# Feed-forward stage of a two-layer encoder: earlier weight requests, a later transpose, and two orders kept

## The chip, the core and the metric

The kernel runs on one core of a Trainium2 chip. The metric is the device time of one execution in microseconds (us). A core has a matrix engine (TensorE, PE in the profile), a vector engine (VectorE, DVE), a scalar engine (ScalarE, ACT), GpSimd (POOL) and SyncE (SP), which issues most DMA transfers, one after the other. Each engine works through its own list of instructions in order; semaphores hold an instruction until what it needs is done.

## The reference, cut to what matters

```
for i in range(2):
    mix = mla_mixer(h) if i == 0 else diff_mixer(h)
    h = layernorm(ALPHA * h + mix)
    h = layernorm(ALPHA * h + (silu(gate) * up) @ w_down)    # gate, up = split(h @ w_gu, 2)
```

Sequence 1024, model width 1024, feed-forward width 2816, all float32. The change lies in the feed-forward part, `silu(gate) * up` and the product with `w_down`, of both layers.

## The kernel before, in words

**The planner.** The kernel is written in a framework that orders the instructions itself: a planner simulates the engines and takes, for each engine, the instruction of the highest priority that is ready by its own clock. Priority is the order in the source, raised by `tc.high_priority`. `behind(i, j)` adds an edge without a semaphore: `i` comes after `j` in the order of the engine that both are on. Buffers come from pools with a number of slots for each tag; a load waits for a slot. The large tiles (tag `big`) have 6 slots, shared by raw gate weights (`gr`), results of the first gate products (`pg`), `hp` and `sh`, which hold finished units on their way to DRAM.

**Precision.** TensorE multiplies in a rounded form. Each operand is split in a high part (a cast on ScalarE) and a low part (a subtraction on VectorE or GpSimd), and a product is three matmuls: high by high, low by high and high by low. `op_unit` (L508 to L516) makes such a pair for a weight; the pairs of the gate stage rotate through tags `wh` and `wl`, 3 slots each. A product of 128 x 512 by 512 inner elements is 4 x 3 = 12 matmuls (`product`, L547 to L557).

**The gate stage** (`ffn` from L521). There are 22 units n, in `order`, each a 128-column block of gate or up weights and its products. The 2 x 2 block product is done in seven products instead of eight, by sums and differences of blocks. Products "1" and "2" go to accumulator `ga`, "6", "7" and "4" to `gb`, "5" and "3" to `gc`. Their inputs are xo, t1, t2, t3, t4 and b22, made of the transposed activations. For units 0 to 5 products "1" and "2" come first, from weights loaded separately (`load_pre`, `gates`), and their results `pg` of units 2 to 5 go to DRAM and come back into `tmp` (L655). The others follow in `stream`: for units 0 and 1 products 5, 3 and then 6, 7, 4; for units 2 to 5 the products 6, 7, 5, 4, 3; from unit 6 on 1, 6, 2, 7, 5, 4, 3. `prepare(n, pr)` forms a weight (sums and differences on VectorE, L585 to L593) and splits it; `consume(n, pr)` does the product, and then VectorE adds the accumulator to the unit's partial sums (L633 to L645), which frees the accumulator for the next product. `prepare` runs 4 positions of the stream ahead of `consume` in the source; the planner may run it further ahead. `load(n)` (L559 to L563) fetches a unit's raw weights, 1024 KB.

**Before the gate stage.** The last row block of the attention output is normalised, transposed on TensorE and put into the block sums by `raw_x` (L463 to L486). That is left over as `pending`, and called inside `ffn` at high priority (L690), after the first `gates(0)`.

**The down stage** (from L737 on) multiplies the finished units with `w_down` in seven blocks, each of 132 matmuls (`whole`, L843), their operands coming from `from_h` and from `b11`, `t1`, `t2` and others. `t2` forms two differences on VectorE for each of 11 steps (L805).

Until the change, only the last unit's products (n = 21) are kept in source order on TensorE (L555).

Of the kernel before, what the change touches and what calls it, by code (L numbers as in the profile page):

```python
# [12 lines left out]
ALU = mybir.AluOpType  # L13
# [3 lines left out]
P = 128  # L17
# [25 lines left out]
def trunk(  # L43
# [103 lines left out]
    def tr(ps_out, in_):  # L147
        T.transpose(ps_out, in_, ident)

# [135 lines left out]
    def out_proj(side, w_o, o_dram, x_src, x_dst, lng, lnb, xo):  # L285


        with tc.tile_pool(name="op0", bufs=2, side=side, reuse_waits="tile") as pool:
# [21 lines left out]
            for tb in LAST_ORDER:  # L310
# [34 lines left out]
                prev = (tb, y)  # L345
        return lambda: raw_x(prev[1], xo, prev[0], f"a0_{prev[0]}")

    class OutProj:
# [95 lines left out]
        def rest(self, lng, lnb, xo):  # L444
# [15 lines left out]
            self.st.close()  # L460
            return lambda: raw_x(self.z[prev], xo, prev, f"a1_{prev}")

    def raw_x(y, xo, tb, name):  # L463

# [56 lines left out]
    def ffn(side, xo, xst, pending, layer, x_src, x_dst, lng, lnb, next_x, spare=()):  # L521
# [25 lines left out]
        def product(n, o, w, x, first):  # L547
            for k in range(4):
                kc = slice(k * P, (k + 1) * P)
                for a, b in ((0, 0), (0, 1), (1, 0)):  # L550
# [14 lines left out]
        def load_pre(n, eng):  # L565
# [4 lines left out]
            for i, pr in enumerate("12"):  # L570
                ops[n, pr] = op_unit(t[:, i], eng, f"gp{layer}_{n}_{pr}")

        begun = set()

        def prepare(n, pr):


            if n not in begun:
                begun.add(n)
                load(n + 1)  # L580
                if n < npre - 1:
                    load(n + 2)
            a11, a12, a21, a22 = (r[n][:, i] for i in range(4))
            if pr == ("5" if n < 2 else "6"):
                V.tensor_tensor(a21, a21, a22, ALU.add)  # L585
            if pr == ("3" if n < 2 else "6"):
                V.tensor_tensor(a11, a21, a11, ALU.subtract)
            if pr == "3":
                V.tensor_tensor(a12, a12, a11, ALU.subtract)
            s3 = None  # L590
            if pr == "7":
                s3 = wp.tile([P, 2, 512], F32, tag="wr", name=f"s3_{layer}_{n}", bufs=2)[:, 0]
                V.tensor_tensor(s3, a22, a11, ALU.subtract)  # L593
            src, eng = {
# [3 lines left out]
            eng = V if n < 2 else eng  # L598
            ops[n, pr] = op_unit(src, eng, f"g{layer}_{n}_{pr}")

        def consume(n, pr):
# [3 lines left out]
            if pr in "12":  # L605
# [26 lines left out]
            if pr == "6":  # L632
                V.tensor_tensor(u2, p1, acc[n, "b"], ALU.add)  # L633
                for c in acc[n, "cs"] if n < 2 else ():
                    V.tensor_tensor(u2, u2, c, ALU.add)
            elif pr == "7":
                V.tensor_tensor(u3, p1, acc[n, "b"], ALU.add)  # L637
                if n < 2:
                    V.tensor_tensor(u3, u3, acc[n, "cs"][0], ALU.add)
            elif pr == "5":  # L640
                V.tensor_tensor(u3, u3, acc[n, "c"], ALU.add)  # L641
            elif pr == "4":
                V.tensor_tensor(p1, p1, acc[n, "b"], ALU.add)
            else:
                V.tensor_tensor(u2, u2, acc[n, "c"], ALU.add)  # L645
            if pr == ("4" if n < 2 else "3"):
# [69 lines left out]
        gates(4)  # L716
        load(2)
        for u in stream[:2]:
            prepare(*u)
# [44 lines left out]
        def from_h(s, name, tags=tags, late=False):  # L764

            for gi, (j0, j1) in enumerate(thirds):
# [803 lines left out]
```

## Time and profile before

| what | value |
|---|---|
| median of 3 runs | 2277.39 us (2275.31 to 2277.57) |
| profiled execution, its time | 2276.84 us |
| its span, first to last instruction | 2275.1 us |
| mean granted TensorE clock | 0.996 |
| PE busy | 98% of the span |
| DVE, ACT, POOL busy | 69%, 45%, 38% |

Busy is the time in which an engine runs an instruction. In a timeline row the first number is the start in us from the span's start, the second the duration; what stands in brackets at the end is the idle time of that engine ahead of the instruction, and what ended it. `op_g`, `op_gp`, `op_h` and `op_w` are weight or activation pairs; `gr` are raw gate weights. L551 is the matmul of the gate stage, L843 that of the down stage. A row of the stretches view gives the stretch, its length, then for each engine busy time and count of instructions, then the granted clock, the DMA engines' share and GB/s. The gate stage runs from about 443 to 872 us in layer 0, and from about 1624 to 2055 us in layer 1.

### The profile page before, as it was taken

Reading aid. Unit: us, or ns where it says so; the run is one execution under the profiler, and the core shown is the slowest. Engines: PE = TensorE matmul, PEld = TensorE weight load, DVE = VectorE, ACT = ScalarE, POOL = GpSimd, SP = SyncE. Lnnn points to the kernel's source line nnn. Section 1 sums busy time; section 2 is a strip of 40 time slices with the busy share of each in tenths; the row PEclk is TensorE's granted clock in tenths of the full one; section 3 lists DMA queues with packets and bytes.
Section 4 is the critical chain, followed back from the end, with each engine's and each line's share of the span. In section 5 each row is a group of like instructions: output and inputs, shape, how many; then the busy total and the mean of one; then the engine's idle time right before and its main releaser. Section 6 shows DMA issues by size and latency. Waiting matters only on the chain.

```text
span 2275.1 us, 31209 instructions
## 1 busy us (share of the span) xinstructions
PE 2238.8 (98%) x11410; PEld 1915.3 (84%) x11410; DVE 1569.9 (69%) x2848; ACT 1022.1 (45%) x2115; POOL 869.2 (38%) x693
## 2 busy tenths in 40 slices
PE   8999999999999999999999999999999999999998
PEld 8899998887888888888889898987778888888886
DVE  5676665696666667878576667677786656658878
ACT  4455664342333333445465656555432333334444
POOL 2232341113444444656333534322014444445551
PEclk9999999999999999999999999999999999999999
DMA  5010115443535338454311212054343223238453
GB/s 203 14 35 31 51 61 188 145 156 103 183 128 195 125 130 324 176 199 148 103 44 32 70 33 67 20 202 167 111 171 117 92 102 107 100 124 311 164 180 149
DMA packets 110443, 287.77 MB, mean 126 GB/s; under 512 B 8513, under 2 KB 30657, under 8 KB 99793
## 3 DMA queue, kind: packets, MB, share of 16 engines
q1 hardware_dynamic: 105872, 275.35, 34.2%
q0 software_dynamic: 4416, 10.42, 1.7%
q8 instruction: 90, 1.47, 0.3%
q14 instruction: 65, 0.52, 0.1%
HBM read 204.47 MB, written 77.07 MB: 124 GB/s over the span
## 4 chain that ended last, share of the span: by engine, by line
PE 87%; DVE 6%; DMA 3%; issue 2%; ACT 1%; POOL 1%; SPq 0%; DVEq 0%; POOLq 0%; ACTq 0%
PE gb L551 14%; PE gc L551 10%; PE ga L551 8%; PE dw L843 6%; PE zp_a L417 4%; PE s_a L219 4%; PE s_b L219 3%; PE dv L843 3%; PE bp L143 3%; PE bp L145 3%; PE dx L843 3%; PE bp L144 3%; PE dy L843 2%; PE o_a L262 2%; PE o_b L262 2%
## 5 line engine op out<-in xcount | busy, mean ns | idle before, releaser
L514 ACT CAST op_g<-gr 128x512 fp32r<-128x512 f32 x240 | 146.8, 621 | 378.6 <-PE gb L551 185.3
L515 POOL TENSOR_TENSOR op_g<-gr,op_g 128x512 fp32r<-128x512 f32 x104 | 145.7, 1406 | 248.7 <-ACT op_g L514 144.5
L515 DVE TENSOR_TENSOR op_h<-rh,op_h 128x512 fp32r<-128x512 f32 x152 | 169.5, 1144 | 48.3 <-ACT op_h L514 48.3
L551 PE MATMUL ga<-xh_m,op_g 128*128 128x512 f32 x512 | 168.3, 389 | 0.0
L514 ACT CAST op_h<-rh 128x512 fp32r<-128x512 f32 x152 | 92.6, 620 | 152.0 <-PE dx L843 50.4
L843 PE MATMUL dw<-op_w_t,op_h 128*128 128x512 f32 x660 | 151.6, 390 | 0.6 <-DVE op_h L515 0.6
L843 PEld LDWEIGHTS dw<-op_w_t,op_h 128*128 128x128 f32 x660 | 123.6, 188 | 26.8 <-DVE op_h L515 1.4
L515 POOL TENSOR_TENSOR op_w_t<-tt,op_w_t 128x512 fp32r<-128x512 f32 x66 | 101.8, 1551 | 84.5 <-ACT op_w_t L514 83.0
L227 ACT ACTIVATE l_b<-l_b,mx_b 128x256 f32<-128x256 f32 (+7 forms) x128 | 99.4, 777 | 66.8 <-DVE mx_b L222 65.3
L515 DVE TENSOR_TENSOR op_g<-gr,op_g 128x512 fp32r<-128x512 f32 x136 | 112.6, 832 | 16.9 <-ACT op_g L514 16.6
L515 POOL TENSOR_TENSOR op_g<-s,op_g 128x512 fp32r<-128x512 f32 x40 | 55.1, 1376 | 179.5 <-ACT op_g L514 171.4
L551 PE MATMUL gb<-t3h_f,op_g 128*128 128x512 f32 x352 | 117.9, 397 | 5.5 <-DVE tmp L633 5.5
L843 PE MATMUL dx<-op_w_b,op_h 128*128 128x512 f32 x528 | 121.1, 390 | 0.8 <-DVE op_w_b L515 0.8
L1367 POOL TENSOR_SCALAR l_b<-l_b,rb,cst 128x128 f32<-128x128 f32 (+3 forms) x64 | 52.6, 821 | 179.2 <-DVE rb L1366 171.8
L843 PEld LDWEIGHTS dx<-op_w_b,op_h 128*128 128x128 f32 x528 | 98.9, 188 | 22.4 <-DVE op_w_b L515 1.7
L551 PE MATMUL gb<-t4h_f,op_g 128*128 128x512 f32 x352 | 115.7, 390 | 1.3 <-DVE tmp L637 1.3
L551 PE MATMUL gc<-b22h_f,op_g 128*128 128x512 f32 x352 | 115.8, 390 | 0.8 <-DVE tmp L641 0.6
L551 PE MATMUL gb<-t2h_f,op_g 128*128 128x512 f32 x352 | 115.7, 390 | 0.4 <-DVE op_g L515 0.4
L551 PE MATMUL gc<-t1h_f,op_g 128*128 128x512 f32 x352 | 115.9, 390 | 0.0
L551 PEld LDWEIGHTS ga<-xh_m,op_g 128*128 128x128 f32 x512 | 96.2, 188 | 19.9
L143 PE MATMUL bp<-xT_f,h_wb 128*128 128x512 f32 x256 | 100.8, 394 | 0.1
L145 PE MATMUL bp<-xT_f,l_wb 128*128 128x512 f32 x256 | 100.7, 393 | 0.0
(391 smaller groups left out, 6753.5 us busy)
## 6 DMA issues: line engine op xcount, KB each, us to landing
gr<-in_w_gu SPq DMA_DIRECT2D x44, 1024.0 KB, 6.8
rh<-h_dr SPq DMA_DIRECT2D x28, 1024.0 KB, 4.9
h_dr<-sh SPq DMA_DIRECT2D x22, 1024.0 KB, 4.9
h_dr<-hp SPq DMA_DIRECT2D x22, 768.0 KB, 4.1
tt<-in_w_dn SPq DMA_DIRECT2D x44, 256.0 KB, 6.3
wo_dr<-op_pwo SPq DMA_DIRECT2D x16, 512.0 KB, 3.4
z<-xs_dr SPq DMA_DIRECT2D x16, 512.0 KB, 8.2
rw_b<-in_w_dn SPq DMA_DIRECT2D x8, 1024.0 KB, 7.7
```

The source lines that it names most:

```text
L143: T.matmul(ps_out, lh, rh, start=(i == 0), stop=False)
L144: T.matmul(ps_out, lh, rl, start=False, stop=False)
L145: T.matmul(ps_out, ll, rh, start=False, stop=(i == n - 1))
L219: T.matmul(s[:, :w], lh, rh[:, ks], start=(j == 0), stop=(j == len(q_pass) - 1))
L227: ends["exp"] = A.activation(l[:, :n], l[:, :n], AF.Exp, bias=mx, scale=-1.0, accum_out=sm).ins
L262: T.matmul(po[:, c], a, b[:, j % 2, c], start=st, stop=sp_, skip_group_check=True)
L417: T.matmul(m, a[:, h, :], self.wo[h][w][:, c], start=(start and h == heads[0] and a is oh and w == 0), stop=(stop and h == heads[-1] and a ...
L514: turns["hi"] = A.copy(t[:, 0], src).ins
L515: turns["last"] = eng.tensor_tensor(t[:, 1], src, f32(t[:, 0]), ALU.subtract).ins
L551: i = T.matmul(o, w[:, a, kc], x[b][:, k, :], start=(first and k == 0 and (a, b) == (0, 0)), stop=(k == 3 and a == 1), skip_group_check=Tr ...
L843: T.matmul(o, h[:, a, c], w[:, b_], start=(first and (a, b_) == (0, 0)), stop=(last and a == 1), skip_group_check=True,).ins for a, b_ in ...
L1367: G.tensor_scalar(l1[:, :n], l1[:, :n], r[:, 1:2], nlam, ALU.mult, ALU.mult)
```

## The change

It has five parts, all in the feed-forward part or in what it calls.

- **Loads.** `prepare(n)` asks for units n+1 and n+2, and up to unit 3 also for n+3. Before, it asked for n+1, and up to unit 4 also for n+2.
- **Last row block, layer 1.** In layer 1 only the weights of units 0 and 1 are loaded ahead of `gates(0)`, and those of 2 and 3 behind it in the source. The first transpose of each half of the last row block is put behind the last product of `gates(0)`. Unit 3's weight casts on ScalarE come behind the copy of the last "1" product.
- **VectorE's lead.** The operations that form weights go through `formed`, the sums through `added_up`. The first forming operations stand behind the last operation of `raw_x`; from step 10 of the stream on, those of position i+4 stand behind the sum of position i-6.
- **Last units.** The products of units 20 and 21 keep the source's order on TensorE, not only those of 21.
- **Down stage.** `t2`'s differences stand behind the split of the same step's `h`.

```diff
     def tr(ps_out, in_):
-        T.transpose(ps_out, in_, ident)
+        return T.transpose(ps_out, in_, ident).ins
...
-            return lambda: raw_x(self.z[prev], xo, prev, f"a1_{prev}")
+            return lambda after: raw_x(self.z[prev], xo, prev, f"a1_{prev}", after)
...
-                tr(pt[:, k * P:(k + 1) * P], y[:, (4 * kh + k) * P:(4 * kh + k + 1) * P])
+                i = tr(pt[:, k * P:(k + 1) * P], y[:, (4 * kh + k) * P:(4 * kh + k + 1) * P])
+                if k == 0 and after is not None:
+                    behind(i, after)
...
-            V.tensor_tensor(b21, b21, b12, ALU.add)
+            return V.tensor_tensor(b21, b21, b12, ALU.add).ins
...
-                    if n == NFF - 1 and k == 0 and (a, b) == (0, 0) and "product" in ends:
+                    if n >= 20 and k == 0 and (a, b) == (0, 0) and "product" in ends:
                         behind(i, ends["product"])
...
                 ops[n, pr] = op_unit(t[:, i], eng, f"gp{layer}_{n}_{pr}")
+                if layer and n == 3:
+                    behind(turns["hi"], ends["p1"])
 
-        begun = set()
+        begun, summed, allowed = set(), [], []
+
+        def formed(*args):
+            i = V.tensor_tensor(*args).ins
+            if allowed:
+                behind(i, allowed[-1])
...
                 load(n + 1)
-                if n < npre - 1:
-                    load(n + 2)
+                load(n + 2)
+                if n < npre - 2:
+                    load(n + 3)
...
+        def added_up(*args):
+            summed.append(V.tensor_tensor(*args).ins)
...
                 if pr == "1":
-                    A.copy(p1, acc[n, "a"])
+                    ends["p1"] = A.copy(p1, acc[n, "a"]).ins
...
-        for n in range(4):
+        for n in range(4 - 2 * layer):
             load_pre(n, G if n < 2 else V)
         gates(0)
+        for n in range(4 - 2 * layer, 4):
+            load_pre(n, V)
         load(0)
         load(1)
         with tc.high_priority(40):
-            pending()
+            turned = pending(ends["product"])
...
+        allowed.append(turned)
...
+        marks = []
         for i, u in enumerate(stream):
+            if i >= 6 and marks[i - 6]:
+                allowed.append(marks[i - 6])
             if i + ahead < len(stream):
                 prepare(*stream[i + ahead])
             consume(*u)
+            marks.append(summed[-1] if summed else None)
...
                 t = op_unit(src, V, f"h{layer}_{name}_{j}", tags, pool)
+                turns["h"] = turns["last"]
...
                 for i in range(2):
-                    V.tensor_tensor(tt[j][:, i], r, tt[j][:, i], ALU.subtract)
+                    behind(V.tensor_tensor(tt[j][:, i], r, tt[j][:, i], ALU.subtract).ins, turns["h"])
```

In `prepare` and `consume`, `V.tensor_tensor` becomes `formed` in the forming operations and `added_up` in the sums. In layer 0 `raw_x` is called without `after`.

More of the change, by code (lines that the diff above doesn't have):

```diff
@@ L345, in out_proj @@
                 prev = (tb, y)
-        return lambda: raw_x(prev[1], xo, prev[0], f"a0_{prev[0]}")
+        return lambda after: raw_x(prev[1], xo, prev[0], f"a0_{prev[0]}")
     class OutProj:
@@ L460, in rest, with raw_x @@
             self.st.close()
-            return lambda: raw_x(self.z[prev], xo, prev, f"a1_{prev}")
-    def raw_x(y, xo, tb, name):
+            return lambda after: raw_x(self.z[prev], xo, prev, f"a1_{prev}", after)
+    def raw_x(y, xo, tb, name, after=None):
         c = slice((tb % 4) * P, (tb % 4) * P + P)
@@ L580, in prepare @@
                 load(n + 1)
-                if n < npre - 1:
-                    load(n + 2)
+                load(n + 2)
+                if n < npre - 2:
+                    load(n + 3)
             a11, a12, a21, a22 = (r[n][:, i] for i in range(4))
             if pr == ("5" if n < 2 else "6"):
-                V.tensor_tensor(a21, a21, a22, ALU.add)
+                formed(a21, a21, a22, ALU.add)
             if pr == ("3" if n < 2 else "6"):
-                V.tensor_tensor(a11, a21, a11, ALU.subtract)
+                formed(a11, a21, a11, ALU.subtract)
             if pr == "3":
-                V.tensor_tensor(a12, a12, a11, ALU.subtract)
+                formed(a12, a12, a11, ALU.subtract)
             s3 = None
@@ L592, in prepare @@
                 s3 = wp.tile([P, 2, 512], F32, tag="wr", name=f"s3_{layer}_{n}", bufs=2)[:, 0]
-                V.tensor_tensor(s3, a22, a11, ALU.subtract)
+                formed(s3, a22, a11, ALU.subtract)
             src, eng = {
@@ L632, in consume @@
             if pr == "6":
-                V.tensor_tensor(u2, p1, acc[n, "b"], ALU.add)
+                added_up(u2, p1, acc[n, "b"], ALU.add)
                 for c in acc[n, "cs"] if n < 2 else ():
-                    V.tensor_tensor(u2, u2, c, ALU.add)
+                    added_up(u2, u2, c, ALU.add)
             elif pr == "7":
-                V.tensor_tensor(u3, p1, acc[n, "b"], ALU.add)
+                added_up(u3, p1, acc[n, "b"], ALU.add)
                 if n < 2:
-                    V.tensor_tensor(u3, u3, acc[n, "cs"][0], ALU.add)
+                    added_up(u3, u3, acc[n, "cs"][0], ALU.add)
             elif pr == "5":
-                V.tensor_tensor(u3, u3, acc[n, "c"], ALU.add)
+                added_up(u3, u3, acc[n, "c"], ALU.add)
             elif pr == "4":
-                V.tensor_tensor(p1, p1, acc[n, "b"], ALU.add)
+                added_up(p1, p1, acc[n, "b"], ALU.add)
             else:
-                V.tensor_tensor(u2, u2, acc[n, "c"], ALU.add)
+                added_up(u2, u2, acc[n, "c"], ALU.add)
             if pr == ("4" if n < 2 else "3"):
```

## The prediction

> **What bounds the kernel now.** I read the page first, then TensorE's waits, the granted clock around the longest of them, and the timeline of the engine that each waits for.
>
> ```profile
> span 2275.1 us, 31209 instructions
> PE 2238.8 (98%) x11410; PEld 1915.3 (84%) x11410; DVE 1569.9 (69%) x2848; ACT 1022.1 (45%) x2115; POOL 869.2 (38%) x693
> ```
>
> TensorE is busy for 98% of the span, and the change leaves its 11410 matmuls alone. So the change can win only TensorE's idle time, 2275.1 - 2238.8 = 36.3 us, and time at a lower clock. The waits of PE, longest first (total us, times, longest):
>
> ```profile
> PE gb L551 <- DVE tmp L633: 5.5, 2, 2.7
> ...
> PE xTp_a L148 <- DVE z_a L183: 2.0, 1, 2.0
> PE gb L551 <- DVE tmp L637: 1.3, 1, 1.3
> ...
> PE dx L843 <- DVE op_w_b L515: 0.8, 2, 0.5
> ...
> PE gc L551 <- DVE tmp L641: 0.6, 1, 0.6
> PE dw L843 <- DVE op_h L515: 0.6, 2, 0.3
> PE gb L551 <- DVE op_g L515: 0.4, 1, 0.4
> ```
>
> L633, L637 and L641 are the sums that read a product's accumulator. The first row is one wait in each layer, the second is the transpose of the last row block in layer 1, the third lies at the end of layer 0's gate stage. Next comes the clock (the third number from the end of a row; before it each engine's busy time, with its count of instructions, in the order PE, PEld, DVE, ACT, POOL) just behind the three waits of 2 us and more, and behind the one of 1.3 us:
>
> ```profile
> 515.60:520.60 5.00, 5.00 (x15) 3.98 (x16) 2.10 (x4) 0.36 (x1) 0.00 (x0) 0.66 0.24 100
> 1631.60:1636.60 5.00, 5.00 (x20) 4.09 (x21) 2.64 (x5) 3.12 (x7) 0.00 (x0) 0.66 0.94 360
> 1700.50:1705.50 5.00, 5.00 (x15) 3.95 (x16) 2.09 (x4) 0.37 (x1) 0.00 (x0) 0.66 0.46 188
> 846.40:852.00 5.60, 5.60 (x25) 4.64 (x26) 3.20 (x5) 0.62 (x1) 1.58 (x2) 1.00 0.74 256
> ```
>
> Each long wait is followed by a stretch at a mean clock of 0.66 over 5.0 us, so 0.34 x 5.0 = 1.7 us of work is lost on top of the wait. The short wait is followed by 1.00. So the three cost 5.5 + 2.0 + 3 x 1.7 = 12.6 us.
>
> The Trainium skill ("TensorE: Matmul & The Clock Gate", Part 1) lets the clock fall only after an idle window of about 3.4 us; the waits here are 2.0 to 2.7 us and the clock fell all the same, so the trace decides against it. By the page's rule the three would have cost their 7.5 us alone.
>
> **The wait at L633.** VectorE ahead of layer 1's wait, and the queue that issues loads:
>
> ```profile
> 1695.64 1.72 DVE L585 TENSOR_TENSOR gr<-gr 128x512 f32<-128x512 f32 x1 [2.51 <-DMA gr<-in_w_gu]
> ...
> 1699.68 0.68 DVE L633 TENSOR_TENSOR tmp<-tmp,gb 128x512 f32<-128x512 f32 x1
> ```
> ```profile
> 1688.82 0.33 SPq L563 DMA_DIRECT2D gr<-in_w_gu  x1
> 1693.15 0.37 SPq L674 DMA_DIRECT2D h_dr<-hp  x1
> ...
> 1698.98 0.35 SPq L563 DMA_DIRECT2D gr<-in_w_gu  x1
> ```
>
> Counting the L585 rows of the layer, one a unit, the L585 at 1695.64 forms unit 5's weights, while TensorE is at unit 2. VectorE works in order and stands there for a load issued at 1688.82. Three forming operations later come the sums (L633) of units 2 and 3, for which TensorE has been waiting. Layer 0 has the same wait, the other of the two.
>
> Two edits meet this. First the limit: stream position of (5,"6") is 25, so it is formed in step 21, behind the sum of position 15, which is (3,"6"); likewise (4,"6") behind (2,"6"). Both L633 then stand ahead of the L585 that blocks. Second the load: unit 5's is now asked for by unit 2's first preparation, ahead of the first `hp` tile, and can take the buffer that is free when the last `pg` tile is stored:
>
> ```profile
> 1669.78 0.33 SPq L682 DMA_DIRECT2D pg_dr<-pg  x1
> ```
> ```profile
> gr<-in_w_gu SPq DMA_DIRECT2D x22, 1024.0 KB, 6.8
> ...
> pg_dr<-pg SPq DMA_DIRECT2D x2, 1024.0 KB, 4.4
> ```
>
> That is 1669.8 + 4.4 = 1674.2 for the issue and 1681.0 for the landing, 14 us ahead of 1695.6. Either edit alone should end this wait: I take the full 5.5 + 2 x 1.7 = **8.9 us** for both layers. What is late next is the sum of unit 2 itself, which needs 0.68 us while TensorE works on unit 3's product.
>
> Does the limit starve TensorE? A product is 12 matmuls, by the row below 12 x 249.6/1099 = 2.7 us.
>
> ```profile
> 550.00:800.00 250.00, 249.60 (x1099) 205.92 (x1098) 167.26 (x202) 84.85 (x146) 108.38 (x79) 1.00 0.42 149
> ```
>
> Converted weights have six buffers, so position m is cast when product m - 6 is done; its forming is held only to the sum of m - 10. That leaves 4 products, 11 us, for 1 to 2 operations of 0.7 to 1.7 us. VectorE is busy 167 of 250 us. I cost the limit at nothing; if that cover went, the price is the wait itself, once a unit. The loads are the same 44, issued earlier: nothing.
>
> **The last row block in layer 1.** Its transposes:
>
> ```profile
> 1631.55 1.09 PE L148 MATMUL xTp_a<-ident,z_a 128*128 128x128 f32 x8 [2.03 <-DVE z_a L183]
> ```
>
> These transposes stand in the middle of unit 0's and 1's four gate products; two of the four, 5.4 us at full rate, are moved ahead of them. The data come 2.0 us after TensorE gets there, so the wait goes with 3.4 us to spare, and the clock's 1.7 with it: up to 3.7 us. The transposes' readers come some 3 us later than now, though, and VectorE is full behind them:
>
> ```profile
> 1635.84:1664.20 28.36, 28.10 (x123) 22.59 (x122) 28.36 (x47) 20.66 (x38) 0.00 (x0) 1.00 0.40 149
> 1664.20:1680.00 15.80, 15.80 (x71) 13.12 (x70) 12.12 (x20) 4.89 (x9) 0.63 (x1) 1.00 0.37 144
> ```
> ```profile
> 1655.69 2.50 DVE L504 TENSOR_TENSOR t4l_f<-xr_m,t4h_f 128x512 fp32r<-128x512 f32 x4
> 1658.10 1.30 DVE L515 TENSOR_TENSOR op_gp<-gp,op_gp 128x512 fp32r<-128x512 f32 x2
> ```
>
> Third group: VectorE is busy for 28.36 of 28.36 us, and TensorE (28.10) waits already for 0.26. The two op_gp at 1658.10 (unit 5's gate weights) are what TensorE needs there; four t4 parts, 2.5 us, go before them and are used last of all the parts. They go first because unit 5's weights come late: its raw buffer waits for unit 3's second half, which waits for the product (0,"2") that is now behind the transposes. With that product early, unit 5's weights land earlier and the planner can take them first. Behind 1664 VectorE has 15.80 - 12.12 = 3.7 us free. The bounds are 0 and 3.7; I take **2.7**, nearer the upper end: the t4 parts alone give 2.5, and other work that isn't needed yet stands before them. The forming behind `turned` and ScalarE's casts behind the copies of p1 only order work that has time: nothing.
>
> **Products of units 20 and 21 in order.** VectorE's sum at the end of the 1.3 us wait in layer 0:
>
> ```profile
> 845.53 0.68 DVE L637 TENSOR_TENSOR tmp<-tmp,gb 128x512 f32<-128x512 f32 x1
> ```
>
> Products 7 and 4 of unit 20 use one accumulator back to back, so the second waits for the sum between them. In program order product 5 lies between, 2.7 us of work against a wait of 1.3: **1.3 us** gone. Unit 21, already in order, shows no such wait. The 0.6 us at L641 (layer 1, in order now) I leave standing.
>
> **Subtractions of t2 behind h.** At most the 0.6 us of `dw`, at least a loss of as much, since the weight then waits instead: nothing.
>
> **Sum.** 8.9 + 2.7 + 1.3 = 12.9 us. A new plan also moves small waits; those of 0.3 to 0.6 us above come to some 2.4 us, and I let the new plan cost 1.0 more. That leaves **11.9 us**. From the profiled execution's 2276.84 (span 2275.1 and 1.7 around it) I get 2264.9. It lies 0.55 below the median of the runs, 2277.39, so for a median: **2265.5 us**.
>
> **Rivals.**
>
> *The start is handed back* (0.12). VectorE's full stretch in layer 1 has no order that helps, and TensorE waits at unit 5's gate weights what it saved: 11.9 - 2.7 = 9.2 us, 2268.2.
>
> *VectorE slows beside GpSimd* (0.10). The limit moves forming out of the stretch before 1674, where GpSimd is all but idle (0.00 and 0.63 in the rows above), into the next, where it works 10.69 us:
>
> ```profile
> 1674.00:1700.00 26.00, 23.67 (x105) 19.29 (x103) 22.30 (x29) 6.59 (x11) 10.69 (x8) 1.00 0.44 152
> ```
> ```profile
> L587 DVE TENSOR_TENSOR gr<-gr 128x512 f32<-128x512 f32 x13 | 17.6, 1353 | 27.1 <-POOL op_g L515 27.1
> ...
> L645 DVE TENSOR_TENSOR tmp<-tmp,gc 128x512 f32<-128x512 f32 x14 | 9.6, 685 | 9.2 <-PE gc L551 9.2
> ```
>
> L587 takes 1353 ns on average where L645 takes 685. By the limit's steps seven forming operations fall in the stretch, as now; with 1.0 us more on each they want 7.0 of the 3.7 us that VectorE has free. The 3.3 us missing plus 1.7 for the clock, in both layers, leave 11.9 - 10.0 = 1.9 us: 2275.5, no change. Against it: some of the seven are that slow already.
> The Trainium skill ("SBUF — State Buffer", on the shared port pair) says that a VectorE operation with two SBUF inputs and a GpSimd one exclude each other for the whole instruction; L645, with one input in PSUM, agrees.
>
> *The change misses one sum* (0.06). The plan still puts something late ahead of L633 in one layer: 4.4 us back, 2269.9; in both, 2274.3.
>
> *The clock falls by itself* (0.03). If the three slow stretches aren't due to the waits, they stay: 5.1 us less, 2270.6. Against it: each follows a wait of 2 us and more, and none stands elsewhere in these two stages. The Trainium skill's longer window (the page and part named above) would speak for it.
>
> *Slower: reloads stand behind loads* (0.08). Loads and the reloads of p1 and g0 share one in-order queue. Unit 4's reload is just in time:
>
> ```profile
> 1723.16 0.69 DVE L633 TENSOR_TENSOR tmp<-tmp,gb 128x512 f32<-128x512 f32 x1 [0.92 <-DMA tmp<-pg_dr]
> ```
> ```profile
> 1726.44 0.39 PE L551 MATMUL gb<-t3h_f,op_g 128*128 128x512 f32 x1
> ```
>
> Its spare time is 1726.44 - 1723.85 = 2.6 us. An earlier load that waits at the queue's head for a buffer held by an `hp` store, as from 1693.15 to 1698.98, would hold it up 5.8 us: 3.2 us of wait and 1.7 of clock, for units 4 and 5 in two layers 19.6 us. Net 7.7 slower, 2285.1. It decides from 2.6 us of delay. Against it: of six large buffers a unit's cycle then needs four for weights, one for hp and one for the sums sent on, which just fits.
>
> **How the numbers follow.** The forecast keeps 0.61. A measurement of this kernel can tell about 0.2%, 4.6 us: faster means below 2272.8. Forecast, handed-back start, one sum missed and the clock give 0.79; I say faster 0.78, same 0.14 (the GpSimd case, two sums missed), slower 0.08. The range: at best every wait named goes (12.6 + 1.3 + 0.6 + 0.6 + 0.8 + 0.4 = 16.3, so 2261.1, and the runs spread by some more); at worst, within 8 in 10, the sums are missed in both layers: 2260.5 to 2274.0.
>
> **What would show it.** Right: no PE wait on L633 over 1 us, granted clock 1.00 through both gate stages, unit 5's L563 near 1674 less 4, L633 ahead of the L585 of the unit two later, transposes of z_a without idle time, no L637 wait at the end of layer 0. Wrong: a stretch at 0.66 anywhere in the gate stages, PE waits for op_gp or op_g of over 1 us, or L633 waiting for tmp<-pg_dr beyond 2.6 us.

## Result and the profile after

| | before | after |
|---|---|---|
| median | 2277.06 us (2275.31 to 2277.57, 4 runs) | 2259.74 us (2258.48 to 2262.6, 4 runs) |
| profiled execution | 2276.84 us, span 2275.1 | 2258.48 us, span 2256.7 |
| mean granted clock | 0.996 | 0.999 |

The ratio is 0.9931, with a 95% interval of 0.9916 to 0.9945: faster by 15.7 us of 2277 (12.5 to 19.1); the medians differ by 17.3. The forecast was 11.9 us less and 2265.5 us. The direction and the places were right, the gain is larger; the median after lies 0.8 us below the lower end of the range.

In the changed kernel the forming operations of VectorE all carry L581 (in `formed`), the sums L613 (in `added_up`), the gate stage's matmul L553, the loads L565, the cast and the subtraction of `op_unit` L516 and L517, the down stage's matmul L865. The head of its page:

```profile
span 2256.7 us, 31242 instructions
...
PE 2231.2 (99%) x11410; PEld 1910.9 (85%) x11410; DVE 1532.1 (68%) x2848; ACT 1023.6 (45%) x2115; POOL 859.2 (38%) x693
```

The span fell by 18.4 us. TensorE's idle time is 2256.7 - 2231.2 = 25.5 us against 36.3, so 10.8 us of that was waiting. The other 7.6 us are in busy time for the same 11410 matmuls: three stretches at half clock that are gone, 3 x 1.7 = 5.1 us, and 2.5 us more. Where the gain lies, by stretches from the first gate product to the first down product, layer 0 and then layer 1, first the kernel before and then the changed one (columns as in the prediction; the third number from the end is the clock):

```profile
443.04:870.93 427.89, 423.19 (x1859) 348.50 (x1858) 294.68 (x379) 151.00 (x262) 159.85 (x117) 1.00 0.43 152
1623.76:2053.96 430.20, 424.52 (x1860) 349.86 (x1858) 285.70 (x364) 143.90 (x249) 165.02 (x118) 0.99 0.35 123
```
```profile
442.60:863.91 421.31, 420.38 (x1859) 347.60 (x1857) 283.48 (x380) 151.48 (x262) 160.69 (x117) 1.00 0.43 155
1614.87:2036.11 421.24, 420.48 (x1859) 347.70 (x1858) 277.99 (x364) 143.77 (x249) 161.56 (x118) 1.00 0.36 126
```

Length less PE busy is the idle time of the stage: 4.70 and 5.68 us before, 0.93 and 0.76 after. The two stages are 6.58 and 8.96 us shorter, 15.5 of the 18.4. PE busy in them falls by 6.85 us, 1.7 more than the three half-clock stretches account for; no view ties that to a place. TensorE's waits in these stages and the down stages, all that the view still shows of 0.2 us and more:

```profile
PE gb L553 <- DVE tmp L613: 1.5, 2, 0.9
...
PE dx L865 <- DVE op_w_b L517: 0.5, 1, 0.5
```

The first row isn't the old wait at L633. It is one wait in each layer, at unit 19, of a product with t4 for the sum of a product with t3, the kind that stood at unit 20:

```profile
820.04 0.47 PE L553 MATMUL gb<-t4h_f,op_g 128*128 128x512 f32 x1 [0.87 <-DVE tmp L613]
```

What ended the wait at L633, layer 1: the queue that issues loads, then VectorE.

```profile
1656.11 0.33 SPq L696 DMA_DIRECT2D pg_dr<-pg  x1
1656.54 4.77 SPq L565 DMA_DIRECT2D gr<-in_w_gu  x2
...
1682.28 0.48 SPq L565 DMA_DIRECT2D gr<-in_w_gu  x1
```
```profile
1681.76 0.68 DVE L613 TENSOR_TENSOR tmp<-tmp,gb 128x512 f32<-128x512 f32 x1
1682.36 3.17 DVE L581 TENSOR_TENSOR gr<-gr 128x512 f32<-128x512 f32 x2
1685.45 0.68 DVE L613 TENSOR_TENSOR tmp<-tmp,gb 128x512 f32<-128x512 f32 x1
```

Counted from unit 0, the loads of units 4 and 5 are the two of the second row; the one at 1682.28 is unit 6's. Unit 5's is issued 0.33 us before that row ends at 1661.3, so 46.1 us after the stage begins; before it was 1688.82 - 1623.76 = 65.1. That is just behind the landing of the last `pg` store (1656.11 + 4.4 = 1660.5, with the prediction's time for such a store), as the prediction had it. On VectorE the sums of units 2 and 3 (L613, at 1681.76 and 1685.45) stand ahead of unit 5's forming, which used to block them and now begins behind 1685.45; the two operations between them form unit 4's weights. Nothing in these rows waits for a load. The last row block's transposes in layer 1 begin without idle time:

```profile
1625.88 1.03 PE L148 MATMUL xTp_a<-ident,z_a 128*128 128x128 f32 x8
```

### The profile page after: what moved, and what is told of

Its sections match the earlier page's. It is cut to its first block, busy times and chain, and to the rows that moved or that the text cites. A ratio compares the mean times of both kernels' runs of the same rounds, so it can differ in the third digit from the quotient of the medians.

```text
span 2256.7 us, 31242 instructions
## 1 busy us (share of the span) xinstructions
PE 2231.2 (99%) x11410; PEld 1910.9 (85%) x11410; DVE 1532.1 (68%) x2848; ACT 1023.6 (45%) x2115; POOL 859.2 (38%) x693
## 4 chain that ended last, share of the span: by engine, by line
PE 96%; DVE 1%; ACT 1%; DMA 1%; issue 0%; POOL 0%; SPq 0%; DVEq 0%; POOLq 0%; ACTq 0%
PE gb L553 16%; PE gc L553 11%; PE ga L553 10%; PE dw L865 8%; PE dx L865 5%; PE zp_a L417 4%; PE s_a L219 4%; PE s_b L219 3%; PE dv L865 3%; PE dy L865 3%; PE bp L143 3%; PE bp L145 3%; PE bp L144 3%; PE o_a L262 2%; PE o_b L262 2%; PE pt_a L148 1%
## 5 line engine op out<-in xcount | busy, mean ns | idle before, releaser
L516 ACT CAST op_g<-gr 128x512 fp32r<-128x512 f32 x240 | 147.9, 622 | 355.5 <-PE gb L553 187.1
L517 POOL TENSOR_TENSOR op_g<-gr,op_g 128x512 fp32r<-128x512 f32 x104 | 142.0, 1369 | 250.3 <-ACT op_g L516 189.9
L517 DVE TENSOR_TENSOR op_h<-rh,op_h 128x512 fp32r<-128x512 f32 x152 | 161.5, 1081 | 75.1 <-ACT op_h L516 75.0
L581 DVE TENSOR_TENSOR gr<-gr 128x512 f32<-128x512 f32 x132 | 121.8, 923 | 85.2 <-POOL op_g L517 85.1
L613 DVE TENSOR_TENSOR tmp<-tmp,gb 128x512 f32<-128x512 f32 x120 | 81.8, 683 | 132.7 <-PE gb L553 128.4
L553 PE MATMUL ga<-xh_m,op_g 128*128 128x512 f32 x512 | 167.7, 389 | 0.0
L516 ACT CAST op_h<-rh 128x512 fp32r<-128x512 f32 x152 | 92.7, 620 | 133.6 <-PE dx L865 38.8
L865 PE MATMUL dw<-op_w_t,op_h 128*128 128x512 f32 x660 | 151.1, 390 | 0.0
L865 PEld LDWEIGHTS dw<-op_w_t,op_h 128*128 128x128 f32 x660 | 123.7, 188 | 25.5
L517 POOL TENSOR_TENSOR op_w_t<-tt,op_w_t 128x512 fp32r<-128x512 f32 x66 | 95.6, 1454 | 98.0 <-ACT op_w_t L516 92.0
L517 DVE TENSOR_TENSOR op_g<-gr,op_g 128x512 fp32r<-128x512 f32 x136 | 116.0, 856 | 17.6 <-ACT op_g L516 17.3
L865 PE MATMUL dx<-op_w_b,op_h 128*128 128x512 f32 x528 | 121.1, 390 | 0.7 <-DVE op_w_b L517 0.5
L865 PEld LDWEIGHTS dx<-op_w_b,op_h 128*128 128x128 f32 x528 | 98.9, 188 | 22.4 <-DVE op_w_b L517 1.4
L553 PE MATMUL gb<-t4h_f,op_g 128*128 128x512 f32 x352 | 115.7, 390 | 1.5 <-DVE tmp L613 1.5
L517 POOL TENSOR_TENSOR op_g<-s,op_g 128x512 fp32r<-128x512 f32 x40 | 55.8, 1395 | 158.9 <-ACT op_g L516 151.4
L553 PE MATMUL gc<-b22h_f,op_g 128*128 128x512 f32 x352 | 115.5, 389 | 0.0
L553 PE MATMUL gb<-t2h_f,op_g 128*128 128x512 f32 x352 | 115.5, 389 | 0.0
L553 PE MATMUL gb<-t3h_f,op_g 128*128 128x512 f32 x352 | 115.2, 389 | 0.0
L553 PE MATMUL gc<-t1h_f,op_g 128*128 128x512 f32 x352 | 115.2, 389 | 0.0
L553 PEld LDWEIGHTS ga<-xh_m,op_g 128*128 128x128 f32 x512 | 96.1, 188 | 19.9
```

The source lines that it names most:

```text
L516: turns["hi"] = A.copy(t[:, 0], src).ins
L517: turns["last"] = eng.tensor_tensor(t[:, 1], src, f32(t[:, 0]), ALU.subtract).ins
L553: i = T.matmul(o, w[:, a, kc], x[b][:, k, :], start=(first and k == 0 and (a, b) == (0, 0)), stop=(k == 3 and a == 1), skip_group_check=Tr ...
L581: i = V.tensor_tensor(*args).ins
L613: summed.append(V.tensor_tensor(*args).ins)
L865: T.matmul(o, h[:, a, c], w[:, b_], start=(first and (a, b_) == (0, 0)), stop=(last and a == 1), skip_group_check=True,).ins for a, b_ in ...
```

## Experiments

The theory is that each wait of the gate stage has a cause of its own and that most parts of the change do their work alone. The rivals are that the parts need each other, and that a wait only moves. The table gives the length of the two gate stages in the profiled execution, measured as above. "Before" and "after" (the changed kernel) in the names tell what an experiment is built on.

| kernel | ratio to before (95%) | layer 0 | layer 1 |
|---|---|---|---|
| before | 1 | 427.89 | 430.20 |
| after | 0.9931 (0.9916 to 0.9945) | 421.31 | 421.24 |
| before + limit | 0.9941 (0.9928 to 0.9955) | 421.28 | 424.69 |
| before + loads | 0.9967 (0.9955 to 0.9980) | 421.43 | 427.74 |
| before + row block | 0.9994 (0.9985 to 1.0003) | 427.07 | 427.45 |
| before + transposes behind only | one run | 428.43 | 427.78 |
| before + order of units 20, 21 | 0.9993 (0.9984 to 1.0002) | 426.87 | 429.68 |
| after - limit | 0.9930 (0.9918 to 0.9942) | 421.84 | 421.59 |
| after - loads | 0.9931 (0.9918 to 0.9945) | 421.04 | 421.49 |
| after - row block | 0.9940 (0.9927 to 0.9954) | 421.22 | 424.72 |
| after - `turned` | 0.9939 (0.9925 to 0.9953) | 421.25 | 422.01 |
| after - order of t2 | 0.9934 (0.9922 to 0.9947) | 421.03 | 421.83 |
| after, order from unit 6 | 0.9946 (0.9934 to 0.9959) | 422.75 | 422.44 |
| after, t3, t1, t4 | 0.9925 (0.9913 to 0.9937) | 420.07 | 421.35 |

Where nothing was changed in a stage its length still differs from the kernel before by up to 0.8 us, and by 1.4 us between two kernels (layer 0 with the row block and with its first edge alone); the ratios are known to about 3 us to each side. So the stages tell more than the ratios, and a small difference counts only where a wait goes with it.

### VectorE's limit alone

On the kernel before, as in the change:

```diff
+            i = V.tensor_tensor(*args).ins
+            if allowed:
+                behind(i, allowed[-1])
...
+        allowed.append(turned)
...
+            if i >= 6 and marks[i - 6]:
+                allowed.append(marks[i - 6])
```

> The kernel before with the limit on VectorE's lead alone. If the order of VectorE caused the two L633 waits, both go and with them both half-clock stretches: about 8.9 us faster than before; the wait at the transposes of z_a (2.0 us and 1.7 us of clock) and the 1.3 us wait at L637 stay. If the late load is what counts, the wait stays at about 2.7 us, at whatever reads unit 5's weights: no gain over 2 us. If VectorE slows beside GpSimd, new waits on op_g of some 3 us stand in the stretch before unit 5.

2263.52 us. TensorE's waits in the two stages:

```profile
PE xTp_a L148 <- DVE z_a L183: 2.1, 1, 2.1
PE gc L551 <- DVE tmp L608: 1.3, 2, 0.7
```

Both waits of the first sum on `gb` are gone, without any load asked for earlier. The kernel holds `turned` too; that edge stands behind `raw_x`, long before the sums of units 2 and 3, and so can't put unit 5's forming behind them. The transposes wait as before. The gain is larger than the 8.9 us expected: the two stages are 6.6 and 5.5 us shorter. The wait of 1.3 us at the end of layer 0 has become one of 0.64 at `gc`, and the one of 0.4 on `op_g` is gone; the rest is not tied to a wait. Layer 0's stage is as short as in the changed kernel.

### The loads alone

On the kernel before:

```diff
-                if n < npre - 1:
-                    load(n + 2)
+                load(n + 2)
+                if n < npre - 2:
+                    load(n + 3)
```

> The kernel before with the earlier requests alone. If the late load caused the L633 waits, unit 5's load is issued some 14 us earlier, VectorE no longer stands at L585, and both waits go: about 8.9 us faster. If it is VectorE's order, L585 to L593 still run ahead of L633 and a shorter wait of 1 to 2 us remains: 3 to 6 us faster. If loads block the queue, L633 waits for tmp reloads by more than 2.6 us and the kernel is slower.

2268.84 us. Its waits:

```profile
PE gb L551 <- DVE tmp L638: 3.1, 3, 1.3
PE xTp_a L148 <- DVE z_a L183: 2.1, 1, 2.1
...
PE gc L551 <- ACT op_g L514: 0.8, 3, 0.3
...
PE ga L551 <- DVE op_gp L515: 0.3, 1, 0.3
PE ga L551 <- ACT pg L616: 0.2, 1, 0.2
```

The L633 waits are gone here too; L638 is the sum between t3 and t4 (1.30 us in layer 0, 0.69 and 1.07 in layer 1). So either edit ends the wait of 8.9 us. But layer 1's stage gains 2.5 us against 5.5 with the limit. Of the difference, 1.1 us are the waits at sums (0.69 + 1.07 against 0.66 at `gc`) and 1.3 the small waits of the last three rows, all in layer 1's start. The changed kernel without the limit, which keeps `turned`, has none of these three. That fits weights that land early while nothing holds VectorE's forming back there, but no run tests it by itself. The comparison flatters the loads: here the wait at the transposes cost no clock (last section), with the limit alone it cost 1.7 us.

### The limit and the loads, each taken out of the changed kernel

The first kernel, then the second:

```diff
-            if i >= 6 and marks[i - 6]:
-                allowed.append(marks[i - 6])
```
```diff
-                load(n + 2)
-                if n < npre - 2:
-                    load(n + 3)
+                if n < npre - 1:
+                    load(n + 2)
```

> The changed kernel without the steps that hold forming behind the sums (forming still stands behind the last row block). If the limit and the earlier loads each end the L633 waits alone, none over 1 us comes back and the time is within 1 to 3 us of the changed kernel, 2260 to 2263 us, the loss in small waits on op_g and op_gp at the start of layer 1 as in the kernel with the loads alone. If the limit is what carries the gain, the L633 waits return with their slow clock: some 9 us slower than the changed kernel.

> The changed kernel with the requests of the kernel before. If the limit suffices, no L633 wait comes back and the time is that of the changed kernel within 1 us. If the limit only moves the blocking L585 behind two sums and the late load then holds up the sums of the next products, a wait of 1 to 3 us stands at L637 or L641 of units 2 and 3 in each layer: 2 to 9 us slower.

2260.22 and 2261.3 us. The waits at the sums, first without the limit, then without the loads:

```profile
PE gb L553 <- DVE tmp L613: 2.5, 4, 0.9
```
```profile
PE gb L553 <- DVE tmp L612: 1.7, 2, 0.9
```

None is longer than 0.9 us, and the waits of 2.7 us don't return. Without the limit two of 0.51 us are added. The two parts do the same work for the long wait; neither is needed while the other stands.

### The row block alone, and its first edge alone

On the kernel before; the second kernel has only the first two hunks:

```diff
+                if k == 0 and after is not None:
+                    behind(i, after)
...
-            pending()
+            pending(ends["product"])
...
-        for n in range(4):
+        for n in range(4 - 2 * layer):
             load_pre(n, G if n < 2 else V)
         gates(0)
+        for n in range(4 - 2 * layer, 4):
+            load_pre(n, V)
...
+                if layer and n == 3:
+                    behind(turns["hi"], ends["p1"])
```

> The kernel before with the last row block of layer 1 alone (transposes behind the first gate products, weights of units 2 and 3 asked for later, casts of unit 3 behind the copy). By the prediction 2.7 us faster, by the full size of wait and clock 3.7; if the start is handed back, PE waits on op_gp of up to 3.7 us appear before the first gc product and the time is within 1 us of before. The L633 waits and their slow clock stay in both layers.

> The kernel before, with nothing but the transposes of the last row block of layer 1 put behind the last product of units 0 and 1; the order of the weights of units 2 and 3 and ScalarE's casts stay as before. Theory (putting the transposes behind is what ends the wait; asking for the weights in another order and holding the casts is what keeps the start from handing it back): no wait at the transposes, no stretch at a lower clock there, but a wait of 1 to 3 us for op_gp or pg at about 1644 to 1662; layer 1's gate stage 427.5 to 430.0 us, against 430.20 before and 427.45 with the whole part alone. Rival (the weights and the casts are worth nothing): the stage within 0.3 us of 427.45. Rival (with the casts not held, the 1.2 us wait at ga of the whole part alone does not come either): 426.3.

2275.69 us, and 2276.13 for the single run of the second. In both the wait at the transposes and the stretch at half clock behind it are gone, and another wait takes part of it back. In the first kernel, TensorE:

```profile
1644.14 0.50 PE L553 MATMUL ga<-xh_m,op_gp 128*128 128x512 f32 x1 [1.19 <-ACT pg L617]
```

ScalarE and VectorE ahead of it:

```profile
1637.26 2.18 ACT L505 CAST t1h_f<-xr_m 128x512 fp32r<-128x512 f32 x4 [1.82 <-DVE xr_m L484]
1639.35 2.18 ACT L505 CAST b22h_f<-xr_m 128x512 fp32r<-128x512 f32 x4
1641.43 2.17 ACT L505 CAST t3h_f<-xr_m 128x512 fp32r<-128x512 f32 x4
1643.52 0.57 ACT L617 COPY pg<-ga 128x512 f32<-128x512 f32 x1
```
```profile
1633.41 0.69 DVE L589 TENSOR_TENSOR gr<-gr 128x512 f32<-128x512 f32 x1 [2.70 <-DMA gr<-in_w_gu]
1634.02 0.68 DVE L517 TENSOR_TENSOR op_gp<-gp,op_gp 128x512 fp32r<-128x512 f32 x1
1634.62 0.68 DVE L591 TENSOR_TENSOR gr<-gr 128x512 f32<-128x512 f32 x1
1635.34 0.69 DVE L593 TENSOR_TENSOR gr<-gr 128x512 f32<-128x512 f32 x1
1635.94 0.68 DVE L517 TENSOR_TENSOR op_gp<-gp,op_gp 128x512 fp32r<-128x512 f32 x1
1636.55 0.68 DVE L484 TENSOR_TENSOR xr_m<-xTp_a,xr_m 128x512 f32<-128x512 f32 x1
```

Read from the bottom: `raw_x`'s sum L484 needs the transposes, which end by 1634.45. VectorE takes it at 1636.55, behind three forming operations. ScalarE stands idle for 1.82 us at its head, then casts t1, b22 and t3, and the copy of `ga` that TensorE waits for comes after all twelve. With the first edge alone TensorE waits for the copies twice (1.08 and 0.51 us), and the stage is 0.3 us longer than with the whole part, less than a stage's length can tell: what the load order and the held casts are worth isn't shown.

With the whole part alone layer 1's stage is 2.75 us shorter, the prediction's 2.7; the number agrees, but the 1.0 us that is missing of 3.7 is lost on `ga`, not at unit 5's weights.

### The row block and `turned`, each taken out of the changed kernel

The first kernel, then the second:

```diff
-                if k == 0 and after is not None:
-                    behind(i, after)
...
-        for n in range(4 - 2 * layer):
+        for n in range(4):
...
-                if layer and n == 3:
-                    behind(turns["hi"], ends["p1"])
```
```diff
-        allowed.append(turned)
```

> The changed kernel with the last row block's part taken out: the weights of units 2 and 3 asked for ahead of the first gate products again, no order on the transposes or on the casts; the limit, the loads, units 20/21 and t2 stay as changed. Theory (in the company of the other parts this part is worth the whole 3.7 us, since the wait for op_gp that it made when alone did not come): 2.0 us of wait at the transposes of z_a are back, 1.7 us of clock only if the wait lies inside one clock window; layer 1's gate stage is 2.0 to 3.7 us longer than the changed kernel's 421.24, so 423.2 to 425.0, and the time 2261.8 to 2263.5. Rival (the limit and the loads had removed this wait too): layer 1's stage within 0.5 us of 421.24. Rival of my prediction (it is worth 2.7 because the start hands 1.0 back): 2.7 us or less with the clock's fall present.

> The changed kernel without the one line that puts the first operations that form weights behind the last operation of raw_x (the limit from step 10 of the stream on, and all else, stays). Theory (with the row block's part alone, VectorE took four operations that form weights, one of them waiting 0.68 us for its load, ahead of raw_x's sums; ScalarE's casts of t1, b22 and t3 came late by that, and the copy of ga behind them held TensorE for 1.2 us; it is this one line that keeps that away): forming operations stand between the sums of raw_x on VectorE again, a wait of 0.6 to 1.3 us on ga for the copy to pg near 1635 us, layer 1's gate stage 421.8 to 422.6 us against 421.24, the time 0.5 to 1.5 us longer than 2259.74. Rival (the other load order already makes the weights land too late or too early for that; my prediction had this line at nothing): no such wait over 0.2 us, the stage within 0.3 us of 421.24.

2264.01 and 2262.15 us. Without the row block's part, TensorE:

```profile
1625.92 1.09 PE L148 MATMUL xTp_a<-ident,z_a 128*128 128x128 f32 x8 [2.04 <-DVE z_a L183]
```

The wait is back, and a half-clock stretch of 3.41 us from 1627.06. The stage is 3.5 us longer, and the waits and the clock named account for it: in company the part is worth its full 2.0 + 1.7. Without `turned`, the waits on `ga`:

```profile
PE ga L553 <- DVE xr_m L486: 0.4, 1, 0.4
...
PE ga L553 <- ACT pg L627: 0.2, 1, 0.2
```

VectorE takes forming operations between `raw_x`'s sums again, L484 comes at 1629.31, 2.5 us after the transposes begin (1.7 in the changed kernel), and the stage is 0.8 us longer. In the changed kernel L484 is not held up, and ScalarE's casts begin with no idle time:

```profile
1627.59 0.68 DVE L484 TENSOR_TENSOR xr_m<-xTp_a,xr_m 128x512 f32<-128x512 f32 x1
```
```profile
1628.32 2.20 ACT L505 CAST t1h_f<-xr_m 128x512 fp32r<-128x512 f32 x4
```

### Units 20 and 21 in order, alone; and order from unit 6

The first on the kernel before, the second on the changed one:

```diff
-                    if n == NFF - 1 and k == 0 and (a, b) == (0, 0) and "product" in ends:
+                    if n >= 20 and k == 0 and (a, b) == (0, 0) and "product" in ends:
```
```diff
-                    if n >= 20 and k == 0 and (a, b) == (0, 0) and "product" in ends:
+                    if n >= 6 and k == 0 and (a, b) == (0, 0) and "product" in ends:
```

> The kernel before with units 20 and 21 in order alone. By the prediction the 1.3 us wait of layer 0 goes and the kernel is 1.3 us faster, less than can be told by its time; the trace tells it. If the wait belongs to the last unit that is still free, it moves to unit 19 with about the same length, and nothing is won. No change of the L633 waits.

> The changed kernel with the products of all units from 6 on in the source's order. If the wait at L637 stands at the last unit that is still free, it goes where no unit beside the first six is free, or moves to the border at unit 5: both waits of 0.9 and 0.6 us go and the kernel is up to 1.5 us faster than the changed one. If TensorE needs the freedom to fill for late weights, new waits on op_g appear through the units, 0.3 us or more each: 5 to 15 us slower.

2274.82 and 2263.47 us. The waits of a product for the sum ahead of it, first with the order from 20 alone, then from 6:

```profile
PE gb L551 <- DVE tmp L637: 1.7, 2, 0.9
```
```profile
PE gb L553 <- DVE tmp L613: 4.5, 2, 2.3
```

From 20: 1.3 us in layer 0 became 0.87 at unit 19, and in layer 1 0.64 at `gc` became 0.87 at `gb`. From 6: nothing at units 19 and 20, but 2.27 us at unit 5 in each layer. The wait stands at the last unit that the order leaves free, at each border tried. No run takes the order out of the changed kernel.

### Products with t3, t1 and t4 in turn

On the changed kernel, `ends[n, pr]` being the last matmul of that product:

```diff
-        def product(n, o, w, x, first):
+        def product(n, o, w, x, first, prev=None):
...
+                    if prev is not None and k == 0 and (a, b) == (0, 0):
+                        behind(i, prev)
...
-                product(n, acc[n, "c"], w, xs["t1" if pr == "5" else "b22"], pr == "5" or n < 2)
+                product(n, acc[n, "c"], w, xs["t1" if pr == "5" else "b22"], pr == "5" or n < 2, ends.get((n, "7")) if pr == "5" and n >= npre else None)
+                ends[n, pr] = ends["product"]
...
-                product(n, acc[n, "b"], w, xs[{"6": "t2", "7": "t3", "4": "t4"}[pr]], pr == "6")
+                product(n, acc[n, "b"], w, xs[{"6": "t2", "7": "t3", "4": "t4"}[pr]], pr == "6", ends.get((n, "5")) if pr == "4" and n >= npre else None)
+                ends[n, pr] = ends["product"]
```

> The changed kernel, with two orders on TensorE added from unit 6 on: a unit's first matmul with t1 behind its last with t3, and its first with t4 behind its last with t1, so that two products into the same accumulator never stand back to back with the sum between them; the order of the units among each other stays free up to unit 19. Theory (what is left is a product standing right behind the one whose sum it waits for; the order between t3 and t4 is all that is needed, and the full order from unit 6 failed because it moved the same meeting to the last free unit): the waits of 0.87 and 0.65 us at unit 19 are gone in both layers and none of over 0.5 us comes in their place; gate stages 420.4 and 420.6 us, the time 1.5 us below the changed kernel's 2259.74, 2258.2. Rival (the meeting moves once more, to unit 5, the last without the order, as when the full order began at unit 6): a wait of 0.6 to 2.3 us near 557 and 1732 us, stages 421 to 422.8, 2259.7 to 2262.7.

2259.53 us. No wait at a sum is left in either layer; layer 0's stage, 420.07, is the shortest of all kernels. In layer 1 two waits come in its place:

```profile
PE ga L553 <- ACT pg L631: 0.6, 1, 0.6
...
PE ga L553 <- ACT pg L629: 0.2, 1, 0.2
```

They lie at units 0 to 5, where the edges don't reach: ahead of the first copy ScalarE waits 3.17 us for the load of unit 2's or 3's weights (2.17 in the changed kernel); why that load came later was not followed. Layer 1 stays as it was, and the medians of 2259.53 and 2259.74 can't be told apart.

### t2's differences as they were

On the changed kernel:

```diff
-                    behind(V.tensor_tensor(tt[j][:, i], r, tt[j][:, i], ALU.subtract).ins, turns["h"])
+                    V.tensor_tensor(tt[j][:, i], r, tt[j][:, i], ALU.subtract)
```

> The changed kernel without the order of t2's differences in the down stages. By the prediction no difference. By the waits of the kernels run so far (0.3 to 0.8 us on op_h in each layer's dw, none in the changed kernel) 0.6 to 1.4 us slower, to be seen in the span between the first dx and the end of the down stages rather than in the median.

2262.19 us. The wait is back:

```profile
PE dw L865 <- DVE op_h L517: 0.6, 2, 0.3
```

It is 0.31 us in layer 0 and 0.26 in layer 1, and the down stages are 0.85 and 0.58 us longer than in the changed kernel. Of the 0.85, 0.48 is a wait at `dx` for `op_w_b`; it also stands in kernels that keep this edge (without the limit, without the loads), so nothing ties it to the edge.

## Why the prediction was right, and where a size was off

**The wait at L633** (8.9 us): right, and by both edits singly, as the step said. Unit 5's load was to come near 1670, 46 us after the stage's begin; measured from there it came at 46.1. That both waits cost 1.7 us of clock as well was so in the kernel before, but the last section shows it to hang on where a wait falls.

**The limit at nothing, and GpSimd.** Right: no wait for `op_g` over 0.2 us came. The rival in which VectorE slows beside GpSimd fell, and it went the other way. The forming groups of the kernel before, and then of the changed one:

```profile
L587 DVE TENSOR_TENSOR gr<-gr 128x512 f32<-128x512 f32 x44 | 53.8, 1223 | 43.3 <-POOL op_g L515 43.2
...
L589 DVE TENSOR_TENSOR gr<-gr 128x512 f32<-128x512 f32 x44 | 42.8, 972 | 21.0 <-POOL op_g L515 20.8
...
L585 DVE TENSOR_TENSOR gr<-gr 128x512 f32<-128x512 f32 x44 | 41.6, 946 | 17.5 <-DMA gr<-in_w_gu 17.5
```
```profile
L581 DVE TENSOR_TENSOR gr<-gr 128x512 f32<-128x512 f32 x132 | 121.8, 923 | 85.2 <-POOL op_g L517 85.1
```

The same 132 operations take 121.8 us in place of 138.2, and L585's 17.5 us of waiting for loads are gone.

**The last row block: the step that was mis-sized.** The prediction took 2.7 of 3.7 us, letting the start hand 1.0 back through a full VectorE at the weights `op_gp`. Taken out of the changed kernel the part costs 3.5 us. By length alone that can't be told from 2.7; but the wait of 2.04 and one half-clock stretch come back with it, and in the changed kernel no wait of 0.2 us stands at layer 1's start, so nothing is handed back there. A hand-back exists, 1.2 us in the part alone, but by another way: forming ahead of `raw_x`'s sums, and through ScalarE to a copy of `ga`. The edge that prevents at least part of it is the one costed at nothing, "the forming behind `turned`": without it 0.6 us of waits and 0.8 of the stage come back. VectorE was full there, as the row of 28.36 of 28.36 us said; the question was which of its work others waited for.

**Units 20 and 21**: 1.3 us forecast. In the profiled executions the waits at these sums went from 1.3 + 0.6 to 0.87 + 0.65, so 0.4 us. The step took the order of one unit to end the meeting of t3 and t4; it moved it to unit 19. Even the 0.4 can't be put down to the order: alone it took 1.94 us of these waits to 1.74, and the limit alone, without it, leaves 1.30.

**t2**: forecast at nothing between bounds of 0.6 each way. It is the upper bound, 0.6 us of waits (and up to 1.4 us by the length of the two down stages, of which 0.48 is the wait at `dx` that nothing ties to this edge).

**The new plan's 1.0 us** was not paid. The small waits fell instead: the 0.4 at `op_g` is gone, and the 0.8 at `dx` is down to 0.5. The latter comes and goes between kernels without a cause that was found.

**The sum.** By the waits: 8.9 + 3.7 + 0.4 + 0.6 + 0.4 + 0.3 = 14.3 us, inside the measured 12.5 to 19.1. Against the forecast of 11.9 that is 1.0 for the plan, 1.0 for the row block, 0.6 + 0.4 + 0.3 for small waits, less 0.9 for the order. That the forecast lies as near as it does is partly luck: the order, taken too high, made up for some of what was taken too low. The profiled pair shows 18.4; the remaining 4 us lie in TensorE's busy time and in stages that the change doesn't touch (start and attention differ by 1.5 us), and no experiment settles them.

## What to carry to other kernels

On an engine that works in order, look for the instruction at the head that waits for something late, and for what is queued behind it; holding it back and bringing its data earlier are two cures for the same wait, and they don't add. When a step is costed at "full engine, so it is handed back", ask which of the work on that engine others wait for: one edge that sorts it gave most of the rest back here. An order that is fixed for the last units only moves a meeting of two products to the last unit left free; order the pair that meets, not the units. Here that ended the waits at sums, and a gain in the time could not be told.

## What the runs showed of the clock

The prediction's rule, a wait of 2 us or more costs 1.7 us of clock, is too simple. In every trace each half-clock stretch but the one at the run's end lasts 3.413 us, and in the kernel before their starts (516.527, 1632.685, 1700.952) are 327.0 and 20.0 such lengths apart: they lie on a fixed grid. Windows of that grid (in each kernel counted from a half-clock stretch of its own trace) around the transposes' wait, in the kernel before and then with the loads alone, around unit 5's wait with the order from 6, and around the wait at L633 in layer 0 with units 20 and 21 in order alone:

```profile
1629.27:1632.68 3.41, 1.38 (x11) 1.13 (x10) 2.82 (x4) 1.58 (x3) 0.90 (x1) 1.00 0.99 339
1632.69:1636.10 3.41, 3.41 (x9) 2.63 (x8) 1.20 (x3) 2.62 (x6) 0.00 (x0) 0.50 0.95 351
```
```profile
1620.75:1624.16 3.41, 2.68 (x12) 1.88 (x10) 2.97 (x6) 0.78 (x2) 0.93 (x1) 1.00 0.73 234
1624.16:1627.57 3.41, 2.08 (x13) 1.88 (x14) 2.56 (x3) 0.81 (x2) 0.00 (x0) 1.00 0.94 339
1627.57:1630.98 3.41, 3.41 (x16) 2.82 (x15) 1.16 (x2) 2.99 (x6) 0.00 (x0) 1.00 0.90 317
```
```profile
1730.53:1733.94 3.41, 1.68 (x7) 1.41 (x8) 2.37 (x4) 1.14 (x2) 2.12 (x2) 1.00 0.00 0
1733.94:1737.35 3.41, 3.41 (x16) 2.83 (x16) 2.72 (x5) 0.62 (x1) 0.42 (x1) 1.00 0.00 0
```
```profile
512.61:516.02 3.41, 1.48 (x6) 1.24 (x7) 3.38 (x6) 0.00 (x0) 0.01 (x1) 1.00 0.97 329
516.02:519.44 3.42, 3.42 (x9) 2.64 (x8) 0.87 (x2) 0.54 (x1) 0.00 (x0) 0.50 0.05 19
```

A wait of 2.03 us inside one window left TensorE busy for 1.38 of 3.41 us, and the next window ran at half clock. A wait of 2.06 us that two windows shared left 2.68 and 2.08 busy, and cost no clock; nor did 2.28 us shared so that 1.68 was left; 1.48 left was followed by half clock. So what counts in these stages is how much of one window is idle, and the limit lies between 1.73 and 1.93 us: the same wait of 2 us costs 2.0 or 3.7 us by where it falls. Of the 15 waits of 2 us and more in the gate stages of all kernels, 12 cost clock; that all three of the kernel before did is in part chance. For the attention's smaller matmuls it lies elsewhere: with the limit alone a window with waits of 1.4 us in all was followed by half clock, from 1545.78. The Trainium skill ("TensorE: Matmul & The Clock Gate", Part 1) calls the window free-running and 3413 ns long, and the traces agree; it asks for an idle window, and here one that was 43% busy was enough.
